# Hybrid mLSTM and Hyena block: the opening stage written out in a fixed order per engine

## The chip, the cores and the metric

One NeuronCore of a Trainium2 chip runs the whole layer in one launch. The metric is the device time of an execution in microseconds (us), lower is better. Engines are named as in the profile: PE (matmul), PEld (its weight loads), DVE (VectorE), ACT (ScalarE), POOL (GpSimd) and SP, whose queue issues nearly all loads.

## What is computed

One layer over 512 latent tokens of width 1024, with a context of 256 tokens that passes through the same weights. Only the start of it is touched by the change: the adaptive modulation, the first RMSNorm, and the first products with it.

```python
mod = silu(c) @ w_ada + b_ada            # 6 * D_MODEL values, for c and for c_ctx
h = rmsnorm(x, norm1_g) * (1 + scale) + shift     # x: (512, 1024), scale and shift from mod
p = h @ lp["w_in"][:, :Q_OFF] + lp["b_in"][:Q_OFF]       # keys, values, gates
p = h @ lp["w_in"][:, Q_OFF:] + lp["b_in"][Q_OFF:]       # queries, output gate, Hyena, merge gates
k = (a @ lp["hy_w4"]).reshape(n, HY_ORDER, 2, H_WIDTH) * window   # Hyena filters, a = sine network of the positions
```

The same `h` is formed for the context with its own modulation. After it come the mLSTM, the Hyena convolutions, the merge, a second norm and a SwiGLU.

## The kernel before

Every large product is made of three matmuls: a weight or an activation is split into a high part and a low part, and `mm3` (L217) adds high x high (L218), high weight x low input (L219) and low weight x high input (L220). The high part is one ACT instruction, the low part one DVE subtraction. Activations lie with features on the 128 partitions, so `x` is 8 tiles of 128 features by 512 tokens.

**The opening stage** stands in `build` from about L994 to L1135 and computes, in this order of dependence:

- the squares of the 8 tiles of `x` on ACT (L384, L387), their running sum on DVE (L388), four short matmuls for the sums (L391), the power -0.5 on POOL (L376) and the broadcast of the result by matmuls (L378). DVE then scales the tiles of `x` (L1044, L1105);
- the modulation. `w_ada` for shift and scale comes in two halves of 16 loads each (`ada_load`, L313): half 0 serves tiles 0 to 3 of `x` (and the context's), half 1 serves tiles 4 to 7. For each half `ada_first` runs 32 short matmuls into four column groups (L322), ACT copies the result (L328), two transposes (L331) and five small DVE instructions (L338, L339) give `modT` and `amod`;
- the modulated tiles `hTh` (ACT, L1075) and `hTl` (DVE, L1080 and L1081);
- the first four query tiles (`NQ` = 4), whose weights `wr` are split by `early_split` into `wh` (ACT, L1051) and `wl` (DVE, L1054). Their matmuls run in two parts of four input tiles each (`part`), 48 matmuls of 512 columns in each part;
- the sine network of the Hyena filters (`filter_network`, three steps of one matmul pair, six DVE instructions L410 to L415 and a sine on ACT L417), and the whole of the first filter spectrum (`sp0`: L448 and L449, DVE L450 to L454, 36 matmuls of 256 columns, L487 to L492);
- the context's sums (`csums`, seven DVE additions L388 of 256 columns, matmuls L391), their broadcast, the scaled context (L1131) and its modulated form `hb` (L1075, L1078, L1081).

**After it** `v_head(h)` for h = 0 to 3 computes values from all six token blocks, four from `x` (`hTh`, `hTl`) and two from the context (`hb`): 144 matmuls for h = 0, L644 to L646. `next_spectrum` finishes one filter spectrum and opens the next between the heads.

**What sets the order.** Each engine runs its own instructions strictly in the order in which a scheduler placed them, by priorities and by its own estimate of when things are ready. `tc.issue_after(i)` holds the instructions under it back until the scheduler has placed instruction `i`. The opening is written as a mixture of such holds (`ahead(n)` runs n steps of `ada_first`; `e0`, `tr`, `am`, `high`, `low` are marks). SP's queue is in order too, and every load reuses one of eight semaphores, so load n is issued once load n - 8 has landed.

Names in the rows: `uh` and `ul` hold `x`, `K` holds half of `w_ada` first and the context later, `s` are scratch tiles, `bank` are PSUM banks, `hb` are scratch tiles of several uses.

## Time and profile before

| what | us |
|---|---|
| median of 3 runs | 1224.8 (1224.13 to 1225.32) |
| the profiled execution | 1225.93 |
| its span, first to last instruction | 1224.1 |
| PE busy | 1183.7 (97%) |
| DVE busy | 833.5 (68%) |
| ACT busy | 527.5 (43%) |
| granted PE clock, mean | 0.991 of full |

The profiled execution took 1.83 us more than its span, which lies around the first and the last instruction, and stands 1.13 us above the median. A change of the span is therefore applied to the median as it stands. PE is the engine that the span consists of; the other engines matter where PE waits for them.

### The profile page before, as it was taken

Reading aid. Unit: us, or ns where it says so; the run is one execution under the profiler, and the core shown is the slowest. Engines: PE = TensorE matmul, PEld = TensorE weight load, DVE = VectorE, ACT = ScalarE, POOL = GpSimd, SP = SyncE. Lnnn points to the kernel's source line nnn. Section 1 sums busy time; section 2 is a strip of 40 time slices with the busy share of each in tenths; the row PEclk is TensorE's granted clock in tenths of the full one; section 3 lists DMA queues with packets and bytes.
Section 4 is the critical chain, followed back from the end, with each engine's and each line's share of the span. In section 5 each row is a group of like instructions: output and inputs, shape, how many; then the busy total and the mean of one; then the engine's idle time right before and its main releaser. Section 6 shows DMA issues by size and latency. Waiting matters only on the chain.

```text
span 1224.1 us, 16772 instructions
## 1 busy us (share of the span) xinstructions
PE 1183.7 (97%) x6440; PEld 1015.2 (83%) x6440; DVE 833.5 (68%) x1336; ACT 527.5 (43%) x824; POOL 69.6 (6%) x132
## 2 busy tenths in 40 slices
PE   4999999999999999999989989999999999999997
PEld 2799988888888888888877988889888888888886
DVE  5967797978989999796767887677654344332332
ACT  3764465753545544444664642233422323222221
POOL 0011110100010000101001111000000000000000
PEclk9899999999999999999999999999999999999999
DMA  9645353364243443335656456773442332333312
GB/s 346 245 150 170 134 181 108 134 231 148 77 148 129 139 147 120 121 104 178 213 172 191 154 198 215 264 260 127 132 155 89 100 103 87 99 92 98 95 48 70
DMA packets 60689, 182.74 MB, mean 149 GB/s; under 512 B 8376, under 2 KB 12224, under 8 KB 58432
## 3 DMA queue, kind: packets, MB, share of 16 engines
q1 hardware_dynamic: 53264, 153.34, 38.4%
q0 software_dynamic: 7344, 28.32, 6.3%
q8 instruction: 51, 0.84, 0.3%
q14 instruction: 30, 0.25, 0.1%
HBM read 151.22 MB, written 30.41 MB: 148 GB/s over the span
## 4 chain that ended last, share of the span: by engine, by line
PE 85%; DVE 6%; DMA 5%; ACT 1%; issue 1%; POOL 0%; SPq 0%; DVEq 0%; POOLq 0%
PE bank L218 25%; PE bank L219 25%; PE bank L220 25%; PE bank L645 2%; PE bank L644 2%; PE bank L646 2%; DMA wr<-in_wada 2%; DMA s<-od 1%; DMA wr<-in_wph 1%; PE bank L448 1%; DVE wl L215 1%; PE bank L601 1%; PE bank L449 1%; DMA ul<-in_xT 1%; PE bank L322 1%
## 5 line engine op out<-in xcount | busy, mean ns | idle before, releaser
L218 PE MATMUL bank<-hTh,wh 128*128 128x512 f32 (+1 forms) x952 | 368.4, 389 | 7.9 <-DVE den L949 3.5
L219 PE MATMUL bank<-hTl,wh 128*128 128x512 f32 (+1 forms) x952 | 367.5, 387 | 2.7 <-DVE hTl L1081 2.1
L220 PE MATMUL bank<-hTh,wl 128*128 128x512 f32 (+1 forms) x952 | 366.7, 386 | 0.0
L214 ACT ACTIVATE wh<-wr 128x1024 fp32r<-128x1024 f32 (+1 forms) x167 | 172.1, 1033 | 403.4 <-PE bank L219 195.0
L215 DVE TENSOR_TENSOR wl<-wr,wh 128x1024 fp32r<-128x1024 f32 (+1 forms) x167 | 197.9, 1188 | 176.6 <-ACT wh L214 175.1
L218 PEld LDWEIGHTS bank<-hTh,wh 128*128 128x128 f32 x952 | 179.7, 189 | 43.0 <-issue 5.9
L219 PEld LDWEIGHTS bank<-hTl,wh 128*128 128x128 f32 x952 | 179.9, 189 | 37.3 <-DVE hTl L1081 2.5
L220 PEld LDWEIGHTS bank<-hTh,wl 128*128 128x128 f32 x952 | 179.9, 189 | 35.5
L219 PE MATMUL bank<-big,wh 128*128 128x512 f32 (+1 forms) x266 | 94.8, 356 | 0.3 <-DVE big L215 0.3
L218 PE MATMUL bank<-big,wh 128*128 128x512 f32 (+1 forms) x266 | 94.7, 356 | 0.0
L220 PE MATMUL bank<-big,wl 128*128 128x512 f32 (+1 forms) x266 | 94.6, 356 | 0.0
L357 DVE SCALAR_TENSOR_TENSOR wr<-wr,crow 128x1024 f32<-128x1024 f32 x32 | 38.9, 1220 | 29.4 <-DMA wr<-in_wada 29.2
L219 PEld LDWEIGHTS bank<-big,wh 128*128 128x128 f32 x266 | 50.3, 189 | 7.9 <-DVE big L215 0.8
L218 PEld LDWEIGHTS bank<-big,wh 128*128 128x128 f32 x266 | 50.3, 189 | 7.1
L220 PEld LDWEIGHTS bank<-big,wl 128*128 128x128 f32 x266 | 50.3, 189 | 7.1
L214 ACT ACTIVATE hb<-hb 128x512 fp32r<-128x512 f32 (+1 forms) x49 | 36.7, 767 | 32.1 <-DVE hb L453 18.1
L1537 DVE TENSOR_TENSOR s<-s,bank 128x512 f32<-128x512 f32 x22 | 15.1, 686 | 46.4 <-PE bank L220 46.4
L215 DVE TENSOR_TENSOR hb<-hb,hb 128x512 fp32r<-128x512 f32 (+1 forms) x49 | 40.4, 860 | 1.8 <-ACT hb L214 1.6
L646 PE MATMUL bank<-wh,hTl 128*128 128x256 f32 (+1 forms) x128 | 36.4, 285 | 0.0
L644 PE MATMUL bank<-wh,hTh 128*128 128x256 f32 (+1 forms) x128 | 36.4, 284 | 0.0
L645 PE MATMUL bank<-wl,hTh 128*128 128x256 f32 (+1 forms) x128 | 36.4, 284 | 0.0
L376 POOL TENSOR_TENSOR rr<-rv,negh 128x2 f32<-128x2 f32 (+1 forms) x6 | 5.6, 925 | 509.6 <-DVE rv L374 509.6
(377 smaller groups left out, 2190.7 us busy)
## 6 DMA issues: line engine op xcount, KB each, us to landing
wr<-in_win SPq DMA_DIRECT2D x64, 512.0 KB, 3.6
wr<-in_w SPq DMA_DIRECT2D x60, 512.0 KB, 3.6
wr<-in_wada SPq DMA_DIRECT2D x32, 512.0 KB, 4.1
Kd<-K POOLq DMA_DIRECT2D x8, 1024.0 KB, 4.8
K<-Kd SPq DMA_DIRECT2D x8, 1024.0 KB, 5.8
wr<-in_wv SPq DMA_DIRECT2D x8, 512.0 KB
gmd<-s POOLq DMA_DIRECT2D x16, 256.0 KB, 2.6
wr<-in_wph SPq DMA_DIRECT2D x8, 512.0 KB, 3.5
```

The costliest lines, as they stand in the source:

```text
L214: act.activation(hi, x, AF.Copy)
L215: dve.tensor_sub(lo, x, hi.bitcast(F32))
L218: pe.matmul(o, wh, xh, start=first, stop=False)
L219: pe.matmul(o, wh, xl, start=False, stop=False)
L220: return pe.matmul(o, wl, xh, start=False, stop=last)
L322: m = pe.matmul(ps[32 * g : 32 * g + 32, :256], silc[:, k, :], units[k, g], start=bool(k == 0), stop=bool(k == KT - 1))
L357: dve.scalar_tensor_tensor(w, w, 1.0, crow[:], op0=ALU.mult, op1=ALU.mult, accum_out=s)
L448: pe.matmul(ps[:], lhs, w4h, start=True, stop=False)
L644: pe.matmul(o, xh, wh, start=bool(k == 0), stop=False)
L645: pe.matmul(o, xh, wl, start=False, stop=False)
L646: m = pe.matmul(o, xl, wh, start=False, stop=bool(k == KT - 1))
L1537: dve.tensor_tensor(t[:], t[:], pb[:], op=ALU.mult)
```

## The change

It rewrites the opening. A context manager `in_order()` records all instructions written under it and chains those of each engine (SP included), so that they are issued in the order of the text. Two such blocks hold the opening; what is not in one (the first spectrum's start, the weights of `v_head 0`) is placed by the scheduler as before.

- SP's first loads are `x`, with the small vectors `vecs` before the last quarter, then `mats`, the 16 loads of half 0, the four query weights, the network's inputs `net`, half 1 and the context. Before, `vecs`, `bgb` and `net` came ahead of `x`, and the first query weight ahead of the last four loads of half 0.
- The query weights are split in two halves of four input tiles (`early_hi`, `early_lo`). The 96 early matmuls are no longer `mm3` triples: for tiles 0 to 3 of `x` all products with `hTh` (both weight parts) of a query tile come first, the products with `hTl` later, between the steps of half 1. Two of the first four `hTh` are made by DVE instead of ACT.
- The sine network's first step now comes after the first modulation, on PE, DVE and ACT; the second during half 1, the third in the second block. `bias_prepare` (five small DVE instructions) moves there too.
- The first spectrum is no longer finished in the opening: it is opened after it and finished behind `v_head 0`.
- The matmuls for the context's sums stand between the `hTl` products of the second and the third query tile.

The core of the diff (the functions `modulated` and `norm`, which only wrap a call, and the renamed returns of `ada_first` are left out):

```diff
+    @contextmanager
+    def in_order():
+
+        traced = nc.cur_bb.bb.instructions
+        n, last, ends = len(traced), {}, []
+        yield ends
+        for i in traced[n:]:
+            if i.engine in last:
+                tc.add_manual_dep(
...
+            last[i.engine] = i.name
+        ends.extend(i for i in traced[n:] if i.name in last.values())
...
+    def bias_prepare(p):
+        dve.tensor_scalar_mul(mngh[:], mng, 0.5)
+        dve.tensor_scalar_mul(bhalf[:], bin_, 0.5)
...
-                if half == 0 and (kp, a) == W0:
-                    dma(raws[0][:, :1024].rearrange("p (a b) -> p a b", a=KT), I["win"][FT_Q])
...
+    def early_q(i, ks, w, x):
+
+        for k in ks:
+            count[i] += 1
+            m = pe.matmul(qps[i][:], early[i][w][:, k], hT[x][k][:], start=count[i] == 1, stop=count[i] == 3 * KT)
...
+    with in_order() as ends:
...
+        for k in KA:
+            norm(k)
+        ahead(4)
...
+        ms = [modulated(k, k > 1) for k in KA]
+        early_hi(0, A)
+        for k in (2, 3, 0, 1):
+            next(ms[k])
+        early_hi(1, A)
+        early_lo(0, A)
+        next(ms[0])
+        early_lo(1, A)
+        next(ms[1])
+        early_q(0, (2, 0, 3, 1), 0, 0)
+        early_q(0, KA, 1, 0)
+        early_q(1, KA, 0, 0)
+        early_q(1, KA, 1, 0)
...
+        network = filter_network(PH, net)
+        next(network)
+        early_q(2, KA, 0, 0)
+        early_q(2, KA, 1, 0)
+        ada = ada_first(PH, 1, units[1], "s2")
+        ahead(1)
+        early_q(3, KA, 0, 0)
+        early_q(3, KA, 1, 0)
+        ahead(2)
+        for k in KB:
+            norm(k)
...
+        early_q(0, KA, 0, 1)
+        ahead(1)
+        next(network)
+        early_q(1, KA, 0, 1)
...
+        early_q(2, KA, 0, 1)
+        early_q(3, KA, 0, 1)
...
+    opened = ExitStack()
+    for i in ends:
+        opened.enter_context(tc.issue_after(i))
+    with in_order():
+        for k in KB:
+            for i in range(NQ):
+                early_q(i, (k,), 0, 0)
+                early_q(i, (k,), 1, 0)
+            if k == 5:
+                next(network)
+                bias_prepare(PH)
+        csums, cb_ = bank(), bank()
+        for k in range(KT - 1):
+            sq_sums(ac_, cxt[k], k, 2, PH, "s2", csums)
+        early_q(0, KB, 0, 1)
+        early_q(1, KB, 0, 1)
+        sq_sums(ac_, cxt[KT - 1], KT - 1, 2, PH, "s2", csums)
+        early_q(2, KB, 0, 1)
         stack = next(network)
...
+        early_q(3, KB, 0, 1)
         rms_bcast(csums[:, :2], 2, cb_, PH, "s2")
...
+    open_spectrum = [spectrum(*sp.pop(0), (dec, skip, (w4s[:, 0], w4s[:, 1])))]
+    for _ in range(2):
+        next(open_spectrum[0])
...
-        v_head(PH, h, v_weights(h))
+        weights = v_weights(h)
+        with behind():
+            v_head(PH, h, weights)
+        opened.close()
```

What moves on the engines, at the places that the next sections speak of.

**PE around the context's sums.** `bank_532` and `bank_521` are the sums, `bank_347` and `bank_283`, `bank_284` are query tiles, `bank_617` is the first spectrum, `bank_669` is `v_head 0`. Before:

```order
L220 MATMUL bank_347<-hTh_492,wl_371 128x512
L391 MATMUL bank_532<-mats_71,s_39_133 128x1 x2
L218 MATMUL bank_347<-hTh_498,wh_370 128x512
L219 MATMUL bank_347<-hTl_499,wh_370 128x512
L220 MATMUL bank_347<-hTh_498,wl_371 128x512
```

After the change, the rows from the last product of the second query tile on:

```order
L1056 MATMUL bank_282<-hTl_456,wh_300 128x512
L402 MATMUL bank_521<-mats_70,s_69_193 128x1 x2
L1056 MATMUL bank_283<-hTl_450,wh_327 128x512
L1056 MATMUL bank_283<-hTl_452,wh_327 128x512
L1056 MATMUL bank_283<-hTl_454,wh_327 128x512
L1056 MATMUL bank_283<-hTl_456,wh_327 128x512
L1056 MATMUL bank_284<-hTl_450,wh_334 128x512
```

Before, nine query matmuls and then the 36 of the first spectrum followed the sums; now eight query matmuls and then `v_head 0` do.

**DVE ahead of the last addition of the context's sums.** `s_39` and `s_69` are the running sums, `hb_559` the first spectrum's low parts, `wl_655` and `wl_662` weights of `v_head 0`. Before:

```order
L215 TENSOR_TENSOR hb_559<-hb_419,hb_558 128x1024
L388 TENSOR_TENSOR s_39_133<-s_39_133,s_143_535 128x256
L388 TENSOR_TENSOR s_39_133<-s_39_133,s_144_538 128x256
L388 TENSOR_TENSOR s_39_133<-s_39_133,s_145_541 128x256
L388 TENSOR_TENSOR s_39_133<-s_39_133,s_146_544 128x256
L388 TENSOR_TENSOR s_39_133<-s_39_133,s_147_547 128x256
L388 TENSOR_TENSOR s_39_133<-s_39_133,s_148_550 128x256
L215 TENSOR_TENSOR hb_559<-hb_419,hb_558 128x1024
L388 TENSOR_TENSOR s_39_133<-s_39_133,s_149_553 128x256
L215 TENSOR_TENSOR wl_697<-wr_695,wh_696 128x1088
```

After the change, the end of `bias_prepare` and the additions:

```order
L293 TENSOR_TENSOR cb_131_501<-vecs_69 128x16
L294 TENSOR_TENSOR cb_131_501<-vecs_69 128x24
L295 TENSOR_TENSOR cb_131_501<-cb_131_501,vecs_69 128x40
L399 TENSOR_TENSOR s_69_193<-s_69_193,s_134_524 128x256
L399 TENSOR_TENSOR s_69_193<-s_69_193,s_135_527 128x256
L230 TENSOR_TENSOR wl_655<-wr_653,wh_654 128x1088
L399 TENSOR_TENSOR s_69_193<-s_69_193,s_136_530 128x256
L399 TENSOR_TENSOR s_69_193<-s_69_193,s_137_533 128x256
L399 TENSOR_TENSOR s_69_193<-s_69_193,s_138_536 128x256
L399 TENSOR_TENSOR s_69_193<-s_69_193,s_139_539 128x256
L230 TENSOR_TENSOR wl_662<-wr_660,wh_661 128x1088
L399 TENSOR_TENSOR s_69_193<-s_69_193,s_140_552 128x256
```

Two weights of `v_head 0` now stand inside the chain of additions; right ahead of it stand `bias_prepare` and, before that, the network's third step; the first spectrum's work, which stood there, has moved behind it.

**ACT between the context's sums and the modulated context.** After the change:

```order
L1059 ACTIVATE gx_117_448<-bank_283,vecs_69 128x512
L428 ACTIVATE hb_341<-hb_341 128x512
L229 ACTIVATE wh_936<-wr_935 128x1024
L432 ACTIVATE astack_563<-hb_341 64x512
L433 ACTIVATE s_142_564<-hb_341 64x512
L1059 ACTIVATE gx_117_448<-bank_284,vecs_69 128x512
L1026 ACTIVATE hb_588<-K_181,modT_75,amod_90 128x256 x2
L1030 ACTIVATE K_181<-K_181,modT_75,amod_90 128x256 x2
```

`gx_117` is the copy of the third query tile, so ACT now stands behind matmuls that come after the sums; `wh_936` belongs to `v_head 1`, and before the change the network's last sine and `astack` were done in the early part of the opening.

## Rows read from the trace of the kernel before

**Rows 1.** busy time by stretch: length, then busy us (xinstructions) per engine, granted clock, DMA

```profile
33.30:100.00 66.70, 66.68 (x462) 59.12 (x463) 52.77 (x92) 41.75 (x67) 5.21 (x9) 0.97 0.53 182
```

**Rows 2.** timeline, SP: start us, us, engine line op out<-in xcount [idle before <-releaser]

```profile
13.53 2.35 SPq L313 DMA_DIRECT2D K<-in_wada  x4
16.24 0.33 SPq L310 DMA_DIRECT2D wr<-in_win  x1
...
24.99 1.95 SPq L313 DMA_DIRECT2D hTh<-in_wada  x4
```

**Rows 3.** timeline from the conditioning matmuls of half 0 to the first wide matmuls

```profile
18.91 1.94 PE L322 MATMUL bank<-hTh,silc 128*32 128x256 f32 x16
...
25.62 2.10 PE L322 MATMUL bank<-K,silc 128*32 128x256 f32 x31
...
28.80 0.43 DVE L415 TENSOR_SCALAR hb<-hb 128x512 f32<-128x512 f32 x1
29.54 0.17 DVE L339 SCALAR_TENSOR_TENSOR amod<-modT,vecs 128x8 f32<-128x8 f32 x1
29.74 1.52 ACT L1075 ACTIVATE hTh<-uh,modT,amod 128x512 fp32r<-128x512 f32 x2 [1.52 <-DVE amod L339]
...
33.32 0.80 PE L219 MATMUL bank<-hTl,wh 128*128 128x512 f32 x1 [2.08 <-DVE hTl L1081]
```

**Rows 4.** timeline, PE: conditioning matmuls of half 1, and two wide matmuls in a row

```profile
45.40 1.07 PE L322 MATMUL bank<-hTh,silc 128*32 128x256 f32 x16
...
51.40 0.39 PE L218 MATMUL bank<-hTh,wh 128*128 128x512 f32 x1
51.62 0.39 PE L219 MATMUL bank<-hTl,wh 128*128 128x512 f32 x1
```

**Rows 5.** timeline, VectorE: first or last of operations that follow on each other

```profile
19.02 0.54 DVE L410 TENSOR_SCALAR hb<-bank,hb 128x256 f32<-128x256 f32 x1 [0.90 <-PE bank L404]
21.17 0.29 DVE L415 TENSOR_SCALAR hb<-hb 128x256 f32<-128x256 f32 x1
...
25.11 0.81 DVE L410 TENSOR_SCALAR hb<-bank,hb 128x512 f32<-128x512 f32 x1 [0.33 <-PE bank L407]
30.76 1.00 DVE L1080 TENSOR_SCALAR s<-uh,amod,modT 128x512 f32<-128x512 f32 x2
32.58 2.50 DVE L1081 TENSOR_TENSOR hTl<-s,hTh 128x512 fp32r<-128x512 f32 x4
...
44.81 1.48 DVE L215 TENSOR_TENSOR dfl<-hb,dfh 128x1280 fp32r<-128x1280 f32 x1
...
66.47 2.40 DVE L1131 TENSOR_TENSOR K<-K,bank 128x256 f32<-128x256 f32 x7
```

**Rows 6.** groups by line and shape, first 70 us, VectorE: count, busy us, mean ns

```profile
L215 DVE TENSOR_TENSOR wl<-wr,wh 128x1088 fp32r<-128x1088 f32 x2 | 2.6, 1291 | 0.2 <-ACT wh L214 0.2
```

**Rows 7.** timeline around the context sums, and the end of v_head 0

```profile
60.49 0.42 DVE L388 TENSOR_TENSOR s<-s,s 128x256 f32<-128x256 f32 x1
60.97 0.61 PE L391 MATMUL bank<-mats,s 128*128 128x1 f32 x4
62.27 0.70 POOL L376 TENSOR_TENSOR rr<-rv,negh 128x2 f32<-128x2 f32 x1 [42.99 <-DVE rv L374]
...
64.27 0.28 PE L218 MATMUL bank<-hb,dfh 128*128 128x256 f32 x1
68.48 0.28 PE L644 MATMUL bank<-wh,hTh 128*128 128x272 f32 x1
70.44 1.09 ACT L1075 ACTIVATE hb<-K,modT,amod 128x256 fp32r<-128x256 f32 x2
...
86.59 0.39 PE L448 MATMUL bank<-wh,astack 128*128 128x512 f32 x1
```

**Rows 8.** timeline, PE, mLSTM stage: the first matmul after an idle time, a later one

```profile
639.13 0.77 PE L218 MATMUL bank<-hTh,wh 128*128 128x512 f32 x1 [3.51 <-DVE den L949]
...
645.23 0.39 PE L220 MATMUL bank<-hTh,wl 128*128 128x512 f32 x1
```

More of the change, by code (lines that the diff above doesn't have):

```diff
@@ L338, in ada_first @@
                 dve.tensor_tensor(o[:, x, y], i[:, x, y], b[:, x, y], op=ALU.add)
-        m = dve.scalar_tensor_tensor(amod[:, fs], modT[:, 1, fs], 1.0, n1g[:, fs], op0=ALU.add, op1=ALU.mult)
-        yield mark.ins, m.ins, copy.ins
+        dve.scalar_tensor_tensor(amod[:, fs], modT[:, 1, fs], 1.0, n1g[:, fs], op0=ALU.add, op1=ALU.mult)
+        yield
     def ada_later(first, last):
@@ L1056, in build @@
-    e0 = early_split(0)
-    with tc.issue_after(next(e0)):
-        tr, am, copy = ahead(8 - AH[0] - AH[1])
-    with tc.issue_after(am):
-        list(e0)
-    dec, skip = spectrum_vectors(PH, *sp[0])
-    dma(w4r, I["hw4"][sp[0]].rearrange("p f n -> p (f n)"))
-    for i in range(1, NQ):
-        dma(raws[i][:, :1024].rearrange("p (a b) -> p a b", a=KT), I["win"][FT_Q + i])
-    dma(fr, I["dftf"])
-    units.append(ada_load(PH, 1, slots[1]))
-    t = T(PH, [128, KT, CTX], F32, "K")
-    dma(t[:], I["cxT"])
@@ L1069, in build @@
-    for k in range(KT):
-        cxt.append(t[:, k])
-    hT = ([], [])
-    def modulate(x, hi, lo, k, i, on_act):
-        a_, b_ = amod[:, k, i : i + 1], modT[:, 0, k, i : i + 1]
-        high = act.activation(hi, x, AF.Identity, bias=b_, scale=a_).ins
-        t = x if on_act else T(PH, [128, 512], F32, "s2")[:, : x.shape[-1]]
-        if on_act:
-            act.activation(t, x, AF.Identity, bias=b_, scale=a_)
-        else:
-            dve.tensor_scalar(t, x, a_, b_, op0=ALU.mult, op1=ALU.add)
-        return high, dve.tensor_sub(lo, t, hi.bitcast(F32)).ins
@@ L1108, in build @@
-    for i in range(AQ):
-        part(i, 0)
-    next(sp0)
-    ada = ada_first(PH, 1, units[1], "s2")
-    tr, am, copy = ahead(8)
-    for i in range(AQ, NQ):
-        part(i, 0)
-    with tc.issue_after(high), tc.issue_after(low):
-        split(fh[:], fl[:], fr)
-    high, low = modulated(1)
-    qb = [T(PH, [128, 512], F32, "cx2")[:] for _ in range(2)]
-    g = T(PH, [128, 2, 512], F32, "gx1", 1)
-    qb += [g[:, 0], g[:, 1]]
-    with tc.issue_after(high), tc.issue_after(low):
-        part(0, 1)
-        csums, cb_ = bank(), bank()
-        for k in range(KT):
-            sq_sums(ac_, cxt[k], k, 2, PH, "s2", csums)
-        next(sp0)
-        part(1, 1)
+            next(ada)
```

187 lines of the change are left out of this document (109 added, 78 removed).

## The prediction, made before the changed kernel was run

> **What bounds the kernel now.** I read the busy time by stretch first. From 33.3 us on PE is busy without a gap (66.68 of 66.70 us to 100 us) [rows 1], so whatever PE loses or wins before that moves the end, and a new idle time of PE inside the opening costs what it lasts. Next the timeline of the opening. PE waits for the first modulation: the last piece of half 0 lands at 24.99 us, since SP's next load, which waits for it, is issued then [rows 2]. The last conditioning matmuls run to 27.72, `amod` starts at 29.54, the first `hTh` at 29.74, and the triples then wait for `hTl` until 33.32 [rows 3]. Then the engine that serves PE: VectorE. The last addition of the context's sums ends at 60.91 and the matmul that reads it starts at 60.97 [rows 7]: before the change these were already close. `v_head 0` starts at 68.48, and by 86.59 it and the first spectrum are both done [rows 7]. That last time is the mark against which I hold the changed kernel: at it the same PE work is done in both, and what follows is the same stream.
>
> **The start moves forward.** Four pieces of 256 KB take 16.24 - 13.53 = 2.7 us, 0.68 each [rows 2]. Of what stood ahead of the last piece of half 0, `net` (386 KB), `bgb` (8 KB) and one query weight (512 KB) now stand behind it: 906 / 256 x 0.68 = 2.4 us. The piece lands at about 22.6. From the end of the conditioning matmuls to `amod` it took 29.54 - 27.72 = 1.8 us, of which some 0.3 was the network's DVE instruction that ended at 29.23 [rows 3]; that instruction is now later, so 1.5. Between landing and the end of the matmuls stand two groups of eight instructions: 0.97 each at the slow rate (1.94 for 16) [rows 3], 0.53 at the fast one (1.07 for 16) [rows 4]. If PE is free when the piece lands, `amod` starts at 22.6 + 1.1 + 1.5 = 25.2. If PE runs the whole conditioning at the slow rate (twelve groups 11.6 us and the two norm steps 3.9 after the first piece at about 12.6, hardly an idle moment), it is 27. I take T = 26.0 for the start of `amod`, 3.5 us earlier than before. The first products need `hTh` alone (0.5 us on DVE, 0.72 to 0.8 on ACT [rows 3, 5]), so PE is in wide matmuls from about T + 0.9 = 26.9 and steadily from T + 1.9, where it was 33.3. That is the gain the change reaches for, 5 to 6 us; from it go 0.2 (one matmul done early before) and about 2 for four network matmuls that ran ahead of 33.3 and now run behind it: at best 3.7 us.
>
> **What DVE has to do from T on.** DVE is in order, so I add up all that stands between the first `amod` and the last addition of the context's sums, by distances between starts: 0.60 for a 512-column subtraction or product (2.50 for four, the last lasting 0.69), 0.46 for a 512-column scale and shift (1.00 for two) [rows 5].
> - two `hTh` 0.9, eight halves of `wl` 4.8, eight pairs of scale and subtraction 8 x 1.25 = 10.0 (the second waits for the first, hence more than 1.06);
> - `modT`, `amod` of half 1 0.6, four norm products 2.4, `dfl` 1.4 [rows 5];
> - the network: 21.46 - 19.02 = 2.44 for a step of 256 columns, twice, and 29.23 - 25.11 less one foreign product 0.6 = 3.5 for the last [rows 3, 5], 8.4 in all. Before the change all three lay ahead of T and cost nothing;
> - `bias_prepare` 0.6, hidden before behind the loads; seven additions at 0.33 (2.40 for seven of that size [rows 5]) 2.3; two weights of `v_head 0` that now stand between the additions, 1.21 each (1.29 less the overlap [rows 6]) 2.4.
>
> Together 33.8; with 0.2 from `amod` to its first reader and 1.0 of waits for ACT (the second `hTh` set, and `wh_661`, whose place on ACT is behind two query copies) 35.0. The same list before the change held about 9 us of the first spectrum instead of network, `bias_prepare` and the two weights (12 us). So the last addition ends at T + 35 = 61.0: no earlier than the 60.91 of before, though T is 3.5 us earlier.
>
> **When PE comes there.** The second `modT` stands on DVE behind both network steps and all `wl`: T + 18.2. With 0.6 for it and `amod` and 1.0 until the first `hTh` is written, PE starts the second part at T + 19.6 whether it was fast or slow before (its own work until then, 44 wide matmuls at 0.227 [rows 4], 32 short ones 3.6, the network 1.0, is 14.6, or 17 with ten at half rate). Then come 40 wide matmuls, 9.1, and the third network step 0.9: PE stands before the sums at T + 29.7 = 55.7. **It waits 5.3 us there**, a wait that is not in the trace of before.
>
> **From the sums to the mark.** PE goes on with 0.46 (60.97 to the next matmul) and eight wide matmuls. ACT's copy of the third query tile waits for four of them, and behind that copy in ACT's queue stand the network's last sine, `wh_936` and two `astack` instructions, behind these on DVE `wl_937`, `astack` and the small step to POOL. Priced by 512-column ACT instructions of 0.6 to 0.76 [rows 3] and double for `wh_936`, that is 3.5 to 4.5; DVE 0.8, POOL 0.7 [rows 7] with 0.3 to pass on; broadcast 0.5. The scaled context begins 7 to 8.5 us after the sums; then 16 ACT instructions at 0.545 (1.09 for two [rows 7]) 8.7, and the split of the spectrum's weights 0.6. PE meets that split inside the fifth block of `v_head 0`, at T + 35 + 17 to 18.7 = T + 52 to 53.7; its own matmuls bring it there at T + 51 to 53. Left to the mark are 8 matmuls at 0.23, 43 at 0.126 ((86.59 - 68.48) / 144) and 36 at 0.117 ((68.48 - 64.27) / 36) [rows 7]: 11.5. The mark is reached at T + 63.5 to 65.2 = 89.5 to 91.2, against 86.59: **2.9 to 4.6 us later, 3.8 taken**. The spectrum's later steps on ACT and DVE (exponentials, sums, splits) run within half a us of PE by the same addition; I put nothing for them.
>
> Every load of `v_head 0` is issued when its `wr` tile is free, some 5 us earlier than PE wants it by the pace of [rows 2]; loads cost nothing, unless the late `wg` piece (last of the six) holds `wh_654`, which has 5 us of room. POOL has no new place.
>
> **The clock at the new wait.** After 3.51 us of idle in the mLSTM stage the next matmuls ran 0.43 apart until 645.2, some 14 of them and 2.8 us lost [rows 8]. Five us at the sums should bring the same. In the sum it only fills the time in which ACT and DVE prepare the context, the difference between the two ends above. The Trainium skill, page "TensorE: Matmul & The Clock Gate", Part 1, says that an idle PE falls back to half clock and regains the full one only under renewed work; taken by itself it would put 2.8 us on top (6.6 later), and the row agrees with the fall; that it adds to this sum, no row shows.
>
> **Rivals.**
> - *PE does not wait at the sums* (faster). Then the opening keeps the 3.7 us: 1221.1. It needs DVE to be at the last addition by T + 29.7 and the context chain to be equally shorter. For it speaks that T may be 25.2. Against it: DVE would have to do its 33.8 us in 29, and each of its distances is read from rows of the same shape. It tips to a gain once DVE's list is under about 31 us and T at 25.2.
> - *The two cancel* (same). T at 25.2 and a list 2 us shorter than mine: mark at 86.7 to 88.5, 1225 to 1226.7.
> - *More is lost* (slower). T at 27, and half clock plus the late context run one after the other, not beside each other: mark at 93 to 95, 1231 to 1233.
> - *The loads do not come earlier*, because eight are in flight at once and share: the piece lands at 24 instead of 22.6, T at 27.4: 1230. This lies inside the forecast's range.
>
> **How the numbers follow.** The profiled execution, 1225.93, is its span 1224.1 and 1.83 around it; 3.8 makes the span 1227.9, and on the median of 1224.8 it makes 1228.6. The chance of the forecast's mechanism (DVE late at the sums, a net loss of 2.5 to 6.5) is 0.63, of more loss 0.05, of cancelling 0.17, of the gain 0.15. A measurement of this kernel tells changes of about 0.2%, 2.4 us, from none: slower 0.66, same 0.18, faster 0.16. T moves the result by 0.9 either way, DVE's list by 1.5; the range for 8 in 10 goes down into the gain's case and up to the edge of the larger loss: 1221.3 to 1232.5. The forecast alone would be 1226.5 to 1231.
>
> **What would show it.** Right: `amod` starts between 25 and 27; DVE without a gap from there to about 61; the sums' matmul starts after an idle time of PE of 4 to 6 us whose releaser is DVE's addition, near 61, no earlier than before; the first `v_head` matmul at 63 to 65.5 with the first spectrum still to come; a second, short wait of PE for ACT in the fifth block. Wrong: the sums' matmul before 58 us, or PE waiting for loads in half 1, or PE busy throughout from 27 us, which would make it faster.

## The result, and the profile after

The changed kernel takes **1230.3 us** (median of 7 runs, 1227.7 to 1231.8) against 1225.3 of the kernel before beside it: ratio **1.0036, interval 1.0024 to 1.0048**. A second measurement, with a second trace, gave 1.0040 (1.0026 to 1.0053). It is slower, by 0.36 to 0.40%; the forecast was 3.8 us, or 0.31%. Executions of one and the same kernel lie 3 to 8 us apart, so ratios with their intervals, and times at fixed points of the trace, are compared below. The profiled execution took 1230.3, its span is 1228.5.

The opening first. SP's loads: the third `hTh` piece of half 1 waits for the last of half 0, so its issue marks that landing: 24.99 us before [rows 2], 21.19 now.

```profile
16.45 2.36 SPq L1084 DMA_DIRECT2D wr<-in_win  x4
19.17 0.33 SPq L1085 DMA_DIRECT2D hb<-in_net  x1
...
21.19 0.33 SPq L324 DMA_DIRECT2D hTh<-in_wada  x1
```

PE's timeline (start, duration, what ended its idle time): the conditioning matmuls end at 22.26, the first wide matmul starts at 24.51 and the stream goes on from there. In [rows 3] it became steady at 33.32.

```profile
18.64 3.62 PE L333 MATMUL bank<-K,silc 128*32 128x256 f32 x32
...
24.51 1.58 PE L1056 MATMUL bank<-hTh,wh 128*128 128x512 f32 x4 [1.33 <-DVE hTh L1024]
...
52.04 1.97 PE L1056 MATMUL bank<-hTl,wh 128*128 128x512 f32 x8
59.09 1.01 PE L402 MATMUL bank<-mats,s 128*128 128x1 f32 x4 [5.07 <-DVE s L399]
59.96 3.52 PE L1056 MATMUL bank<-hTl,wh 128*128 128x512 f32 x8
63.32 0.29 PE L654 MATMUL bank<-wh,hTh 128*128 128x272 f32 x1
...
67.73 0.71 PE L389 MATMUL bank<-mats,rr 128*128 128x128 f32 x4 [0.72 <-POOL rr L387]
```

The row to see is the one at 59.09: PE has finished the `hTl` products of the second query tile at 54.02 and stands 5.07 us for VectorE's addition (L399). In [rows 7] the same matmul, at 60.97, waited for nothing. And the eight matmuls behind the wait take 3.36 us from 59.96 to 63.32, 0.42 each, where two in a row stand 0.22 apart in [rows 4]. VectorE in the same time:

```profile
23.61 0.17 DVE L350 SCALAR_TENSOR_TENSOR amod<-modT,vecs 128x8 f32<-128x8 f32 x1
...
38.49 0.55 DVE L421 TENSOR_SCALAR hb<-bank,hb 128x256 f32<-128x256 f32 x1 [0.52 <-PE bank L415]
...
43.68 0.69 DVE L1034 TENSOR_TENSOR hTl<-s,hTh 128x512 fp32r<-128x512 f32 x1 [0.30 <-ACT hTh L1026]
...
52.97 0.16 DVE L290 TENSOR_SCALAR mngh<-vecs 128x8 f32<-128x8 f32 x1
...
53.56 0.95 DVE L399 TENSOR_TENSOR s<-s,s 128x256 f32<-128x256 f32 x2
54.43 1.28 DVE L230 TENSOR_TENSOR wl<-wr,wh 128x1088 fp32r<-128x1088 f32 x1
55.63 1.87 DVE L399 TENSOR_TENSOR s<-s,s 128x256 f32<-128x256 f32 x4
57.41 1.28 DVE L230 TENSOR_TENSOR wl<-wr,wh 128x1088 fp32r<-128x1088 f32 x1
58.62 0.42 DVE L399 TENSOR_TENSOR s<-s,s 128x256 f32<-128x256 f32 x1
...
66.74 0.16 DVE L385 TENSOR_SCALAR rv<-bank 128x2 f32<-128x2 f32 x1
```

From `amod` at 23.61 to the end of the last addition at 59.04 it is 35.4 us, with idle times of 0.52 us (for PE) and 0.30 us (for ACT) and no others of that size. The two `wl` of `v_head 0` stand inside the additions. By stretch (length, busy time and count of each engine, then the granted clock), to be held against [rows 1], where PE was busy for 66.68 of the same 66.70:

```profile
33.30:100.00 66.70, 60.41 (x415) 52.69 (x414) 52.10 (x105) 39.28 (x66) 5.21 (x9) 0.95 0.46 157
54.00:59.00 5.00, 0.02 (x1) 0.00 (x0) 4.74 (x8) 3.02 (x6) 0.00 (x0) 0.72 0.34 105
59.00:63.40 4.40, 4.31 (x13) 3.60 (x14) 0.72 (x2) 1.35 (x3) 0.00 (x0) 0.54 0.20 60
63.40:67.50 4.10, 3.61 (x29) 3.39 (x27) 2.08 (x4) 3.16 (x5) 0.53 (x1) 1.00 0.67 184
```

PE now lacks 6.3 us of that stretch; the granted clock stands at 0.54 behind the wait, that is near the lower level of 1.2 GHz, and at 1.00 from 63.4 on. Two points measure the sum. The first spectrum and `v_head 0` are done at 93.38, with 35 matmuls of `v_head 1` (12, 12 and 11, at 0.12 us) already among them: 93.38 - 4.2 = 89.2, against 86.59 [rows 7], **2.6 us later**. And the transposes of the mLSTM's gates (L781 before, L791 now), which come behind all four heads and stand alone in the trace, are **3.1 us later** (in their rows the durations in ns come first, then the first and the last start in us):

```profile
93.38 0.40 PE L459 MATMUL bank<-wh,astack 128*128 128x512 f32 x1
...
L781 PE MATMUL bank<-mats,hb x4: 201/202/223, 195.8 to 196.0; 8*128 8x8 f32 x4
...
L791 PE MATMUL bank<-mats,hb x4: 201/202/222, 198.9 to 199.2; 8*128 8x8 f32 x4
```

This point, called *the transposes*, is the yardstick of the experiments: before, 195.8; changed, 198.9, in both its traces.

### The profile page after: what moved, and what is told of

It reads as the page before. It is cut to its first block, busy times and chain, and to the rows that moved or that the text cites. A ratio compares the mean times of both kernels' runs of the same rounds, so it can differ in the third digit from the quotient of the medians.

```text
span 1228.5 us, 16777 instructions
## 1 busy us (share of the span) xinstructions
PE 1186.9 (97%) x6440; PEld 1016.4 (83%) x6440; DVE 835.7 (68%) x1342; ACT 526.5 (43%) x826; POOL 69.7 (6%) x132
## 4 chain that ended last, share of the span: by engine, by line
PE 78%; DMA 8%; DVE 8%; issue 2%; ACT 2%; POOL 1%; SPq 0%; DVEq 0%; POOLq 0%; ACTq 0%
PE bank L233 22%; PE bank L234 22%; PE bank L235 22%; DMA wr<-in_wada 2%; PE bank L1056 2%; PE bank L655 2%; PE bank L656 2%; PE bank L654 2%; DVE wl L230 1%; DMA s<-od 1%; DVE wr L368 1%; POOL rs L973 1%; DMA wr<-in_wph 1%; PE bank L612 1%; PE bank L459 1%
## 5 line engine op out<-in xcount | busy, mean ns | idle before, releaser
L233 PE MATMUL bank<-hTh,wh 128*128 128x512 f32 (+1 forms) x920 | 354.6, 387 | 5.4 <-DVE den L959 3.0
L234 PE MATMUL bank<-hTl,wh 128*128 128x512 f32 (+1 forms) x920 | 353.5, 385 | 0.6 <-DVE hTl L1567 0.6
L235 PE MATMUL bank<-hTh,wl 128*128 128x512 f32 (+1 forms) x920 | 353.3, 385 | 0.0
L233 PEld LDWEIGHTS bank<-hTh,wh 128*128 128x128 f32 x920 | 173.0, 189 | 38.4 <-issue 4.9
L235 PEld LDWEIGHTS bank<-hTh,wl 128*128 128x128 f32 x920 | 173.0, 188 | 33.9
L234 PEld LDWEIGHTS bank<-hTl,wh 128*128 128x128 f32 x920 | 173.0, 188 | 33.4 <-DVE hTl L1567 0.8
```

Source lines behind the costliest of these rows:

```text
L233: pe.matmul(o, wh, xh, start=first, stop=False)
L234: pe.matmul(o, wh, xl, start=False, stop=False)
L235: return pe.matmul(o, wl, xh, start=False, stop=last)
```

## The experiments

All kernels are edits of the changed one. The table has the time, the ratio to the kernel before (interval), the first `amod`, the start of the context sums' matmul with PE's wait before it, and the transposes.

| kernel | median us | ratio (interval) | `amod` | sums, wait | transposes |
|---|---|---|---|---|---|
| before | 1225.3 | 1 | 29.54 | 60.97, 0 | 195.8 |
| changed | 1230.3 | 1.0036 (1.0024, 1.0048) | 23.61 | 59.09, 5.07 | 198.9 |
| e1 | 1226.8 | 1.0015 (1.0005, 1.0026) | 23.30 | 56.12, 3.24 | 195.4 |
| e2 | 1228.9, one run | | 23.58 | 58.84, 5.07 | 199.0 |
| e3 | 1234.2 | 1.0070 (1.0057, 1.0083) | 23.35 | 61.48, 2.95 | 201.1 |
| e4 | 1224.2 | 0.9992 (0.9983, 1.0000) | 23.55 | 53.01, 0 | 195.4 |
| e5 | 1230.4 | 1.0043 (1.0030, 1.0056) | 23.50 | 59.07, 0.15 | 197.2 |
| e6 | 1233.0 | 1.0066 (1.0051, 1.0081) | 26.90 | 62.09, 5.07 | 202.1 |
| e7 | 1232.8 | 1.0070 (1.0052, 1.0088) | 23.51 | 62.75, 5.21 | 202.9 |
| e8 | 1224.8 | 0.9994 (0.9980, 1.0008) | 23.39 | 56.33, under 0.7 | 194.3 |
| e9 | 1224.3 | 0.9992 (0.9977, 1.0007) | 23.24 | 56.06, 0.23 | 191.5 |
| e10 | 1229.6 | 1.0037 (1.0024, 1.0051) | 23.51 | 58.31, 0.27 | 196.5 |
| e11 (e9 again) | 1222.2 | 0.9974 (0.9962, 0.9987) | 23.60 | 56.55, 0.23 | 192.1 |
| e12 (changed again) | 1230.5 | 1.0040 (1.0026, 1.0053) | 23.47 | 58.96, 5.07 | 198.9 |

### What ends the wait: e1 and e2

**e1** takes the two weights out of the additions: their splits are held until the last addition of the context's sums (`adds[-1]`) has been placed.

```diff
...
+        hold[:] = adds[-1:] if h == 0 else []
         weights = v_weights(h)
+        hold.clear()
...
-            split(hi[:, :n], lo[:, :n], raw[:, :n])
+            with ExitStack() as e:
+                if hold:
+                    e.enter_context(tc.issue_after(hold[0]))
+                split(hi[:, :n], lo[:, :n], raw[:, :n])
```

> The two weight splits of v_head 0 (DVE wl_655, wl_662, 2.4 us) are held behind the last addition of the context's sums; all else as in the changed kernel. Theory A (VectorE's list sets the wait at the sums): the list is 2.4 us shorter, the last addition can end at 56.6, and since the last square on ACT, which stands behind the copies of query tiles 0 and 1, ends at 56.0, the sums' matmul starts at about 56.5 instead of 59.09 and PE's wait falls from 5.07 to about 2.5; time 2.6 us under the changed kernel's 1230.3, about 1227.7. Theory B (ACT's last square, not VectorE, ends the wait): 59.1 and 5.1 as before, 1230. Theory C (the wait is only the place where PE shows a delay that is set later, by the context's chain to the fifth block of v_head 0): the wait falls, but the same 2.5 us come back as an idle time of PE between 70 and 80 us, 1230.

**e2** writes the last context square ahead of ACT's copies; `sums_mm` issues the matmuls alone.

```diff
-        for k in range(KT - 1):
-            sq_sums(ac_, cxt[k], k, 2, PH, "s2", csums)
+        for k in range(KT):
+            sq_sums(ac_, cxt[k], k, 2, PH, "s2")
         early_q(0, KB, 0, 1)
         early_q(1, KB, 0, 1)
-        sq_sums(ac_, cxt[KT - 1], KT - 1, 2, PH, "s2", csums)
+        sums_mm(ac_, 2, csums)
...
```

> The last of the eight context squares on ACT is written ahead of the copies of query tiles 0 and 1 (it then is done at about 54.5 instead of 56.0); the order on VectorE is unchanged. Theory A (VectorE's list sets the wait): nothing moves, the sums' matmul starts at 59.1, wait 5.1, time within 0.5 us of the changed kernel. Theory B (the last square on ACT sets it): the sums' matmul starts at about 57.5, wait 3.5.

The sums' matmul of e1 on PE with the seven additions on VectorE, the last square on ACT, and the transposes; then the sums' matmul of e2; last, six of the seven additions of the kernel before:

```profile
56.12 0.60 PE L406 MATMUL bank<-mats,s 128*128 128x1 f32 x4 [3.24 <-DVE s L403]
...
52.47 3.60 DVE L403 TENSOR_TENSOR s<-s,s 128x256 f32<-128x256 f32 x7
...
54.48 0.41 ACT L402 ACTIVATE s<-K 128x256 f32<-128x256 f32 x1
...
L795 PE MATMUL bank<-mats,hb x4: 201/202/225, 195.4 to 195.6; 8*128 8x8 f32 x4
...
58.84 0.97 PE L406 MATMUL bank<-mats,s 128*128 128x1 f32 x4 [5.07 <-DVE s L399]
...
56.38 3.06 DVE L388 TENSOR_TENSOR s<-s,s 128x256 f32<-128x256 f32 x6
```

In e1 the matmul starts at 56.12 (56.5 expected). The wait is 3.24, not 2.5, because PE gets there 1.1 us earlier than in the changed kernel, 0.3 of it from an earlier `amod`. The additions last 3.60, where seven products of that size last 2.40 [rows 5], but not because they stand for ACT: the last square ends at 54.89 and the last addition starts some 0.8 us later. They are 0.53 us apart, as the six in a row of the kernel before are (3.06 in all). Each reads the sum that the one before it has written, and the products don't; that this is the reason was not tested. In e2 the square is early and nothing moves. So VectorE's list ends the wait, in the changed kernel and in e1; in no run here did ACT's square end it. C falls: what the shorter wait wins is still there at the transposes, 3.5 us, and in the time, 3.5 us under the changed kernel's median.

### What the half clock behind the wait costs: e3, e5 and e10

**e3** fills the wait. Three more dependencies, not shown, keep VectorE's and ACT's orders up to the sums as in the changed kernel.

```diff
...
         early_q(1, KB, 0, 1)
+        for j in range(22):
+            pe.matmul(fill_[:], early[0][0][:, 4 + j % 4], hT[0][4 + j % 4][:], start=True, stop=True)
         sq_sums(ac_, cxt[KT - 1], KT - 1, 2, PH, "s2", csums)
...
```

> 22 extra matmuls of 512 columns (22 x 0.227 = 5.0 us) into a PSUM bank that nobody reads stand on PE where it waits for the sums; the orders of VectorE and ACT up to the sums are as in the changed kernel. PE's idle time is filled, not shortened. Theory A (the half clock after the wait is a cost of its own, on top of the idle time): the sums' matmul starts at 59.1 to 59.3 as before, but the eight wide matmuls behind it run 0.227 apart instead of 0.43, v_head 0 starts at about 61.5 instead of 63.32, time 1.6 to 2.0 us under the changed kernel, about 1228.4. Theory B (the slow matmuls only fill time in which the context is not ready anyway, as the forecast's sum had it): v_head 0 starts earlier, but PE idles as much longer at the fifth block, near 76 us: 1230.3.

It doesn't answer the question: the filling matmuls read the weights of query tile 0, and ACT's `wh_654` waits for that buffer. VectorE's two `wl` start late, both waiting for ACT, and the sums with them (61.48):

```profile
54.73 1.29 DVE L230 TENSOR_TENSOR wl<-wr,wh 128x1088 fp32r<-128x1088 f32 x1 [0.72 <-ACT wh L229]
...
59.71 1.29 DVE L230 TENSOR_TENSOR wl<-wr,wh 128x1088 fp32r<-128x1088 f32 x1 [1.90 <-ACT wh L229]
```

**e5** reads the fourth tile's weights instead (`early[3][0]`).

> As e3_filled_wait, but the 22 filling matmuls read the weights of the fourth query tile, whose buffer is not wanted by a weight split of v_head 0 before the sums; in e3 they held the buffer of the first and so delayed wl_655 and wl_662. The orders of VectorE and ACT up to the sums are those of the changed kernel. Theory A (the half clock after the wait is a cost of its own): the sums' matmul starts near 59.1, the eight wide matmuls behind it 0.227 apart, v_head 0 at about 61.5 instead of 63.32, time 1.6 to 2.0 us under the changed kernel, 1228.4. Theory B (the slow matmuls only fill time in which the context is not ready): PE idles as much longer before or inside the fifth block of v_head 0, 1230.3.

The eight matmuls behind the sums, and the granted clock from 59.0 to 63.4, which was 0.54:

```profile
59.51 2.09 PE L1057 MATMUL bank<-hTl,wh 128*128 128x512 f32 x8
...
59.00:63.40 4.40, 4.33 (x28) 4.02 (x29) 1.19 (x2) 2.67 (x4) 0.00 (x0) 1.00 0.31 80
```

With the sums at the same time (59.07), the eight matmuls start 0.24 apart, `v_head 0` starts at 61.44 instead of 63.32, and 1.7 us of it are left at the transposes. So the half clock is a cost on top of the idle time at that point, and B is wrong about the fifth block: PE doesn't idle there. But the time is no shorter, 1230.4. The trace shows where most of the 1.7 us go: to a wait of PE at the mLSTM's first row products, 2.3 us here and 0.5 in the changed kernel. I put that to the additional PSUM bank of the filling, which shifts all later ones.

**e10** writes the filling into the bank of the later broadcast (`cb_` for `fill_`).

> As e5_filled_wait_2, but the filling matmuls write the bank that the broadcast uses later, so no further PSUM bank is taken and the later banks fall as in the changed kernel. In e5 the opening was 1.7 us shorter and the time was not, with a wait of 2.3 us at the mLSTM's first row products (0.5 in the changed kernel). Theory A (the half clock costs 1.7 us, and e5's later wait came from the shifted banks): that wait is 0.5 again, the transposes come at 197.2 (198.9 in the changed kernel), time 1.7 us under the changed kernel, 1228.6. Theory B (the opening's gain is taken back by the mLSTM stage whatever the banks): the wait is 2 us or more, time 1230.3.

PE's waits at the row products, for the changed kernel, e10 and e3, and what ACT waits for ahead of its copies of these rows, for the first two:

```profile
PE bank L875 <- ACT rrow L850: 0.5, 1, 0.5
...
PE bank L876 <- ACT rrow L851: 1.8, 1, 1.8
...
PE bank L876 <- ACT rrow L851: 2.5, 1, 2.5
...
580.13 1.06 ACT L377 ACTIVATE wr<-crow 128x1024 f32<-128x1024 f32 x1 [2.58 <-DMA crow<-in_crow]
...
579.46 1.06 ACT L378 ACTIVATE wr<-crow 128x1024 f32<-128x1024 f32 x1 [4.28 <-DMA crow<-in_crow]
```

The transposes come at 196.5, 2.4 us earlier than in the changed kernel (0.7 more than expected, as the sums themselves came 0.8 earlier), and the wait is still there: the banks were not its cause. The time, 1229.6 and a ratio of 1.0037, is that of the changed kernel. ACT's copies of the rows stand, in order, behind an activation that waits for a load, `crow`; in e10 it starts 0.7 us earlier than in the changed kernel, in which PE reached this place 2.4 us later. The wait goes with the filling and not with a gain of the opening: e3, whose opening is later than that of the changed kernel, has it too (2.5), and e1, e4, e8 and e9, whose openings are earlier, do not (0.5 in each). In the changed kernel SP issues this load 9.0 us behind the one ahead of it, in e3, e5 and e10 10.6 to 11.1 us; why is not settled. So the 1.7 us are shown at the transposes and not in the time of a whole execution.

### Whether the head start is worth anything: e6 and e7

**e6** puts SP's loads back (all but `bgb`, 8 KB), and takes them from their new places.

```diff
+        dma(vecs[:], I["vecs"])
+        dma(net[:, :772], I["net"])
         for q in range(4):
             t = T(PH, [128, 2, SEQ], F32, ("uh", "ul")[q % 2])
             dma(t[:], I["xT"][:, 2 * q : 2 * q + 2])
...
+                if half == 0 and (kp, a) == (3, 0):
+                    dma(raws[0], I["win"][FT_Q])
...
```

> The changed kernel with SP's old order of loads: vecs and net ahead of x, the first query weight ahead of the last four loads of half 0; the order on every other engine is that of the changed kernel. Theory A (the new load order sets T, the start of the first amod): amod starts 2 to 2.5 us later, 25.6 to 26.1 instead of 23.61, and as VectorE's list from there is the same 35.4 us, the sums' matmul follows at 61.2 to 61.7; time 1232.5. Theory B (the conditioning matmuls on PE set T, not the loads): amod stays at 23.6 to 24.2, time 1230.3 to 1231.

**e7** puts the triples back, on PE alone.

```diff
-        early_q(0, (2, 0, 3, 1), 0, 0)
-        early_q(0, KA, 1, 0)
-        early_q(1, KA, 0, 0)
-        early_q(1, KA, 1, 0)
...
         next(network)
+        for k in KA:
+            for i in (0, 1):
+                early_q(i, (k,), 0, 0)
+                early_q(i, (k,), 0, 1)
+                early_q(i, (k,), 1, 0)
         early_q(2, KA, 0, 0)
...
-        early_q(0, KA, 0, 1)
...
-        early_q(1, KA, 0, 1)
...
```

> Only PE's order changes: for tiles 0 to 3 of x the matmuls of query tiles 0 and 1 are triples again (high x high, high weight x low input, low weight x high input, tile by tile), behind the network's first matmul; VectorE, ACT and SP keep the orders of the changed kernel. Theory A (VectorE's list sets the time of the context's sums, so PE's head start is given back there): PE waits some 4 us for hTl between 25 and 33 us, comes to the sums with 1 to 4 us less to wait, and the sums' matmul starts at 59.1 to 59.8; time within 1 us of the changed kernel. Theory B (PE's stream sets the end, so an early start is worth what it lasts): PE's wait at the sums stays near 5 us, the sums' matmul starts at about 63; time 4 us above the changed kernel, 1234.

`amod` and the sums' matmul of e6; then of e7 VectorE's second network step and the sums' matmul:

```profile
26.90 0.17 DVE L352 SCALAR_TENSOR_TENSOR amod<-modT,vecs 128x8 f32<-128x8 f32 x1
...
62.09 1.01 PE L404 MATMUL bank<-mats,s 128*128 128x1 f32 x4 [5.07 <-DVE s L401]
...
42.24 0.55 DVE L421 TENSOR_SCALAR hb<-bank,hb 128x256 f32<-128x256 f32 x1 [4.36 <-PE bank L415]
...
62.75 0.92 PE L402 MATMUL bank<-mats,s 128*128 128x1 f32 x4 [5.21 <-DVE s L399]
```

e6 is theory A, and larger than I had it: T moves by 3.3 us (2 to 2.5 expected), the sums follow 35.2 us behind it with the same wait of 5.07, and the transposes are 3.2 later. The landing of the last piece of half 0, by the mark used above, is at 24.47 here and at 21.19 in the changed kernel. The load order is worth 3.3 us of the start.

e7 is a miss for theory A. The sums are 3.7 us later and the time is 2.5 over the changed kernel's (1230.3), the transposes 4.0. VectorE's list isn't closed in itself: it has the network's second step in it, and that reads a matmul which stands on PE behind the wide ones. VectorE stood for it 4.36 us; in the changed kernel it was 0.52 (the row at 38.49 above). So a head start of PE isn't thrown away at the sums; it is what keeps VectorE's list without gaps. Both parts of the change, loads and order of the products, are worth three to four us each at the transposes; the loss lies in what was moved into the list between T and the sums: with two of those instructions out again, e1 is level with the kernel before there (195.4 against 195.8).

### A version without the wait: e4, e8, e9 and e11

**e4** moves the work behind the sums: the network's third step, `bias_prepare` and, as in e1, the two weights.

```diff
...
-            if k == 5:
-                next(network)
-                bias_prepare(PH)
         csums, cb_ = bank(), bank()
-        for k in range(KT - 1):
-            sq_sums(ac_, cxt[k], k, 2, PH, "s2", csums)
+        for k in range(KT):
+            sq_sums(ac_, cxt[k], k, 2, PH, "s2")
         early_q(0, KB, 0, 1)
         early_q(1, KB, 0, 1)
-        sq_sums(ac_, cxt[KT - 1], KT - 1, 2, PH, "s2", csums)
+        sums_mm(ac_, 2, csums)
         early_q(2, KB, 0, 1)
-        stack = next(network)
         early_q(3, KB, 0, 1)
         rms_bcast(csums[:, :2], 2, cb_, PH, "s2")
         for k in range(KT):
             dve.tensor_tensor(cxt[k], cxt[k], cb_[:, :CTX], op=ALU.mult)
+        next(network)
+        bias_prepare(PH)
+        stack = next(network)
...
```

> The wait's causes are taken away together: the last square on ACT ahead of the copies, the two weight splits of v_head 0, the network's third step and bias_prepare behind the context's sums, and the context's norm (rv, broadcast, eight products) ahead of the network's third step. VectorE's list up to the last addition is 6.4 us shorter and ends at about 52, before PE gets there (53.4). Theory A: no wait at the sums, no half clock behind it, no wait at the broadcast: 5.1 + 2.0 + 0.7 = 7.8 us under the changed kernel, about 1222.5, that is 3 under the kernel before. Theory B (the opening's work on VectorE and ACT only moves its wait): PE idles instead before the context's matmuls or the first spectrum, between 58 and 85 us, 3 us or more are given back, 1225.5 or above.

The sums don't wait, but the transposes are no earlier than in e1. VectorE now has the network between the context's low parts, starts the first spectrum's steps (L469 to L473) at 70.88, and comes only at 76.26, behind them, to the addition `gates` that frees a bank of `v_head 0`. The addition, the wait, and the stretches behind it:

```profile
76.26 0.15 DVE L674 TENSOR_TENSOR gates<-bank,bgb 128x16 f32<-128x16 f32 x1
...
PE bank L662 <- DVE gates L674: 1.8, 1, 1.8
...
76.00:78.00 2.00, 1.44 (x8) 1.47 (x9) 1.58 (x7) 2.00 (x3) 0.96 (x2) 0.76 0.00 1
78.00:80.00 2.00, 2.00 (x11) 2.00 (x11) 1.94 (x2) 1.22 (x2) 0.12 (x1) 0.50 0.38 131
```

PE is idle for 1.8 us, and the granted clock falls to 0.50 after it, the lower level of 1.2 GHz; 15 matmuls then stand 0.225 apart instead of 0.126. Wait and slow matmuls together take back 3.3 us: theory B, in part, and a time of 1224.2 where theory A had 1222.5.

**e8** leaves the network where it is and lets PE's own query matmuls cover the wait. The holds on the weights and the place of `gates` are not shown.

```diff
...
+        for i in range(NQ):
+            early_q(i, KB, 0, 1)
+        sums_mm(ac_, 2, csums)
         rms_bcast(csums[:, :2], 2, cb_, PH, "s2")
         for k in range(KT):
             dve.tensor_tensor(cxt[k], cxt[k], cb_[:, :CTX], op=ALU.mult)
+        stack = next(network)
+        w4s = T(PH, [128, 2, 512], F32R, "hb")
+        split(w4s[:, 0], w4s[:, 1], w4r)
+        bias_prepare(PH)
...
```

> The changed kernel with the wait's causes moved and PE's order too: the sums' matmuls stand behind all query matmuls (16 instead of 8 of 512 columns cover the wait, 1.8 us); the last context square ahead of ACT's copies; the weight splits of v_head 0, and bias_prepare, behind the last addition; the network's third step stays where it is. Behind the sums the context's norm comes first on VectorE, and ACT's splits for v_head 1 and the second spectrum stand behind the context's 16 instructions; the gates' addition that frees a bank of v_head has priority. Theory A: the last addition ends at 55.2, PE gets to the sums at 55.6 and waits less than 0.5 us, no half clock follows, no wait over 1 us until the first spectrum is done: 5.1 + 2.0 us under the changed kernel, about 1223, 2 under the kernel before. Theory B (the opening's work on ACT and VectorE is what fills the time, whatever its order): PE waits 3 us or more at the first spectrum or the context's blocks instead, 1225.5 to 1227.

**e9** goes for e8's two short idle times: on ACT `wh_654` stands behind the last square and the first query copy and ahead of the second, and on PE the broadcast stands behind the 13th matmul of `v_head 0`.

```diff
...
+        if h == 0:
+            for i, j in ((highs[-2], sqs[-1]), (highs[-2], cps[0]), (cps[1], highs[-2]), (highs[-1], cps[2]), (cps[3], highs[-1])):
+                tc.add_manual_dep(i, j.name, ...)
...
+        if h == 0:
+            for i in bc[4:6]:
+                tc.add_manual_dep(i, vm[4].name, ...)
```

> As e8_sums_behind_queries, with the two short idle times of PE taken away that its profile shows: ACT's wh_654 now stands behind the last context square (so the last addition ends near 55.1 instead of 56.3), and the broadcast of the context's norm 12 matmuls later on PE. Theory A (each idle time of PE in the opening, and the slow matmuls behind it, is a cost of its own): PE is busy from 41.5 to 85 us with no wait over 0.5 us and no stretch below full clock; the gates' transposes of the mLSTM, at 195.8 us in the kernel before, 198.9 in the changed one and 194.3 in e8, come at 191 to 191.5; time 3.3 us under e8's, 1221.5, ratio to the kernel before about 0.997. Theory B (what the opening gains is taken back further on, as e8's 1.5 us at 195 us were): the transposes come at 191 but the time stays at 1224 to 1225.

The same two stretches in e8 and in e9, and the transposes in e9 and in its repetition e11:

```profile
57.00:60.00 3.00, 2.54 (x14) 2.10 (x14) 1.42 (x5) 2.95 (x5) 0.70 (x1) 0.87 0.49 145
60.00:63.00 3.00, 3.00 (x17) 3.00 (x16) 2.94 (x8) 3.00 (x7) 0.00 (x0) 0.56 0.20 73
...
57.00:60.00 3.00, 2.76 (x23) 2.74 (x23) 2.06 (x5) 2.92 (x6) 0.70 (x1) 1.00 0.58 164
60.00:63.00 3.00, 3.00 (x26) 3.00 (x26) 2.94 (x8) 3.00 (x6) 0.00 (x0) 1.00 0.65 139
...
L799 PE MATMUL bank<-mats,hb x4: 201/202/223, 191.5 to 191.7; 8*128 8x8 f32 x4
...
L799 PE MATMUL bank<-mats,hb x4: 201/202/224, 192.1 to 192.4; 8*128 8x8 f32 x4
```

In e8, with PE idle for some 0.2 us before 57 and 0.5 of the next 3 us, the clock is at 0.56 from 60 to 63, and the time is 1224.8 where theory A had 1223. In e9 the clock is at 1.00 throughout, and the transposes are 4.3 us ahead of the kernel before. PE is busy from 41.7 to 85 us but for 0.64 us in pieces of 0.2, which is in sum what e8 had: that the clock stayed up because less idle time was left is not shown. The time of e9 didn't show the gain at first (1224.3; 0.9992, interval 0.9977 to 1.0007), as its theory B had it. So e9 and the changed kernel were run once more.

> e9_no_idle once more, for a second trace and more times: at 191.5 us it was 4.3 us ahead of the kernel before, its profiled execution took 1222.24, its median 1224.3. Theory A (the difference between executions arises behind the opening): the second trace has its transposes at 191.3 to 191.7 again, whatever its own time, and the waits that differ lie in the mLSTM stage, 580 to 745 us. Theory B (the opening itself varies, by when its loads land): the transposes move by 1 us or more with the time of the execution. The ratio to the kernel before is 0.9965 if the opening's gain is kept, 0.999 if it is taken back as in the first measurement.

> The changed kernel itself once more, beside e11, for a second trace of it. Theory A (executions differ behind the opening): wait at the sums 5.0 to 5.2, first amod 23.3 to 23.7, transposes 198.6 to 199.1, whatever its time; ratio 1.0036. Theory B (the opening varies): the transposes move by 1 us or more with the time of the execution.

e11 gives 0.9974 (0.9962 to 0.9987): 1222.2 against 1225.3, the first kernel here that is faster than the one before beyond its interval; the first measurement of the same kernel doesn't show it. Its transposes, at 192.1, miss both the 191.3 to 191.7 of theory A and the full microsecond of theory B. The repeated traces agree in the opening, the changed kernel's within 0.1 us and e9's within 0.6, and from there to the end they differ by 0.8 and 1.9 us (span less transposes: 1228.5 - 198.9 = 1029.6 and 1229.3 - 198.9 = 1030.4 for the changed kernel, 1220.5 - 191.5 = 1029.0 and 1219.2 - 192.1 = 1027.1 for e9). So in these four traces the difference arises as much behind the opening as in it, or more. Of 3.7 to 4.3 us won there, the two measurements of e9 keep 1.2 and 3.1; how much stays on average is not settled by them.

## Why the prediction was right, and where its steps were not

- **The mechanism held.** VectorE's list from T to the last addition was forecast as 35.0 us and took 35.4; PE was to stand before the sums at T + 29.7 and stood there at T + 30.4; the wait was to be 5.3 and was 5.07, with VectorE's addition as its releaser. e1 shortens the list and the wait with it, e2 shows that ACT's square doesn't end it, e6 shifts T and carries list and wait along unchanged.
- **The total of the list was closer than its terms.** Additions and the two weights among them were to take 4.7 us and took 5.5 (53.56 to 59.04): the additions were priced by products that stand 0.33 apart, where additions to one running sum had stood 0.53 apart before the change. A wait of 0.52 us for PE was not in the list. Against that, 1.0 us was put down for waits for ACT, and 0.30 came. That these nearly cancel is luck.
- **T was wrong**, 23.61 against 26.0 and outside the 25.2 to 27 given. Two terms: the landing (21.19, forecast 22.6), as the loads moved back were priced at 2.4 us by their bytes and e6 measures 3.3; and the choice of a middle between PE at the fast and at the slow rate, where the conditioning ended 1.07 us behind the landing, the faster case. This alone would have brought the mark of the sum to 87.1 to 88.8. The upper end, 27, also doesn't follow from the terms given for it (12.6 + 11.6 + 3.9 + 1.5 is 29.6), and the trace has 64 conditioning matmuls for half 0, eight groups of eight and not twelve. With T, the sums' matmul was early as well: 59.09 where "near 61, no earlier than before" was the sign of being right.
- **The clock was wrong the other way.** The sum let the half clock behind the wait fill time in which the context wasn't ready. But the context itself waits for those slow matmuls: ACT's copy of the third query tile needs four of them, and what makes the context ready stands behind that copy. With the wait filled and the sums at the same time, the scaled products on VectorE start 1.3 us earlier (the changed kernel, then e5):

```profile
68.48 2.73 DVE L1193 TENSOR_TENSOR K<-K,bank 128x256 f32<-128x256 f32 x8 [1.58 <-PE bank L389]
...
67.20 2.74 DVE L1197 TENSOR_TENSOR K<-K,bank 128x256 f32<-128x256 f32 x8 [1.58 <-PE bank L390]
```

So it is a cost by itself, 1.7 us at the transposes (e5). The Trainium skill, page "TensorE: Matmul & The Clock Gate", Part 1, has the idle engine at half clock until it has worked again; the granted clock of 0.54 behind the wait agrees. The 2.8 us of [rows 8], which the prediction named as what that rule by itself would put on top, were too many in this place.
- **The second wait didn't come.** The scaled context was to hold PE up inside the fifth block of `v_head 0`. PE came to that block at 76.86 without idle time, while ACT was at the last two instructions of the context, done at 76.92: the context was just covered. Its scaled products began 9.4 us behind the sums, where 7 to 8.5 were forecast, and its sixteen ACT instructions took 8.0 us, where 8.7 were forecast, so it was done at T + 53.3, inside the T + 52 to 53.7 of the sum. (The terms given for that sum add up to 16.3 to 17.8 us behind the last addition, not to the 17 to 18.7 that were used.) PE's own stream, with its slow matmuls in it, set the mark, 30.1 us behind the sums' matmul, within the 28.5 to 30.2 of the sum. The block's first matmul on PE and the end of the context on ACT, from the timeline of the changed kernel:

```profile
76.86 0.29 PE L654 MATMUL bank<-wh,hb 128*128 128x272 f32 x1
...
75.84 1.08 ACT L1030 ACTIVATE K<-K,modT,amod 128x256 f32<-128x256 f32 x2
```

- **So the size came out by luck, by two errors of opposite sign**: T was 2.4 us early, and from T to the mark it took 65.6 us where 64.4 was the middle of the sum. That makes 2.6 us late at the mark and 3.1 at the transposes for 3.8 forecast, 4.4 in the ratio's middle. The remaining 1.3 between the transposes and the span's end is as large as the difference between two traces of one kernel, and stays unexplained.
- **The ledger of PE**, by distances between starts: steady wide matmuls begin 8.6 us earlier (24.51 against 33.32 less one matmul) and the mark is 2.6 later, so 11.2 are lost between. The wait is 5.1, the slow rate behind it 1.9, the network's matmuls, which had lain ahead of 33.3 us, 1.3, the broadcast's wait 0.7, the half-1 conditioning with its transposes 1.0; 1.2 are left in small pieces.
- **Of the rivals**, "PE does not wait at the sums" named the right condition. e9 makes it true and is 3.7 to 4.3 us ahead of the kernel before at the transposes, but 1.2 and 3.1 in the time by its two measurements; the rival's price was 3.7. "The loads do not come earlier" is refuted by the landing at 21.19 and by e6.

## What to carry to other kernels

When an opening is pulled forward, add up the in-order list of the engine that feeds the next meeting point, with everything that the pull has moved into it, and compare it with the arrival of the engine that is pulled; a head start is kept only as far as that list shrinks too. Write the links between the lists into the sum: a step of one list that reads a result from far down another's turns a delay there into a delay of both (e7). And price a wait of PE with the slow matmuls behind it, even a short one.

## What the runs showed of the hardware that I had not expected

The granted clock fell behind idle times much shorter than the 3.51 us of [rows 8]: to 0.50 after 1.8 us in e4, and to 0.56 in e8 after some 0.7 us in pieces around 57 us. It stayed at 1.00 after 0.7 us at the broadcast in the changed kernel, after 0.8 us there in e5, and after pieces of 0.2 us in e9 that add up to as much as those of e8. With some 0.7 us of idle time these runs show both outcomes, so no rule is drawn from them.

Additions of 128x256 to one running sum stood 0.53 us apart on VectorE (the kernel before, e1), products of the same size, none of which reads another's result, 0.33 [rows 5]. That the dependence makes the difference is not shown: the products also read one operand from a PSUM bank. A sum of an engine's work should take its distances from rows of the same operation.
